# Hybrid decoder step: the mixers' pauses in units 0, 1 and 7, a late copy of scalars, and the order of small column tiles

## The chip, the cores and the metric

The kernel runs on one core of a Trainium2 chip. A core has TensorE (PE, matrix products; its weight loads are listed as PEld), VectorE (DVE), ScalarE (ACT), GpSimd (POOL) and SyncE (SP, which here issues nearly all transfers). Each runs its own list of instructions in order and waits on semaphores for the others. The metric is the device time of one execution in microseconds; of several runs the median counts.

## What is computed

One layer of a decoder, for 16 learned tokens with 256 prompt tokens, and for 8 single sample tokens that go on from given states: T = 280 columns in all, 264 without the learned tokens.

```python
x = LN1(alpha * x + 0.5 * swiglu(x, f1))          # 2048 -> 5504 -> 2048
x = LN2(alpha * x + mixer(x))
x = LN3(alpha * x + 0.5 * swiglu(x, f2))

# mixer: x @ w_in (2048 -> 10 * 2048), split in q_r, k_r, v_r, g_r, q_h, f, i_h, g_h, a_r, a_h
# retention, 8 heads of 256: rotary q, k; decay gamma_h per step
S_new = gamma * S + k^T v ;  o_r = decayed (q k^T) v + q S
# HGRN2 (gated attention), 16 heads of 128: forget gate f per feature, k = 1 - f
S_new = f * S + k^T v ;      o_h = decayed (q k^T) v + q S
y = (sigmoid(a_r) * silu(g_r) * LN(o_r) + sigmoid(a_h) * silu(g_h) * RMS(o_h)) @ w_out
```

Outputs are y for prompt and sample, and the states of both mixers for both.

## The kernel before

**Products.** Features lie on the 128 partitions, tokens are the moving columns. Each number is split in a high and a low part of a reduced float type, and each 128 x 128 weight block takes three matmuls in `dense` (L217): xh·whi, xl·whi, xh·wlo, in this order. Weights are streamed in units of 8 blocks (512 KB): SP loads `raw` (L184), ScalarE rounds it to `whi` (L187), VectorE subtracts to get `wlo` (L188). raw, whi and wlo have three buffers each, so a weight unit is prepared when PE has left the third before it. A unit is 24 matmuls of L217.

**Stages.** FFN 1 (up, dn); the mixer; the output projection (wo); FFN 2. In the mixer the input projection goes in eight units u = 0 to 7, each with two HGRN2 heads and one retention head: the groups f, q_h, i_h, q_r, k_r, v_r of unit u, and then the gates (g_r with a_r, g_h with a_h, for two column blocks) of unit u − 1. After the gates of unit 7 comes wo.

**The two mixers as threads.** What follows a projection is written as two Python generators, `mix_hg(u)` for HGRN2, started after i_h of unit u, and `mix_ret(u)` for retention, started after v_r. `pump` runs once in each k step of a projection (6 matmuls of L217) and advances the threads: `yield n` means that the thread pauses n steps. So a mixer's small matmuls, its pieces, are strewn between projection matmuls, and what other engines do for them hides behind the projections, if the pause is long enough. PE's order is exactly the order in which this program is written. The orders of VectorE, ScalarE, GpSimd and SP are set by the scheduler of the framework: a pause in PE's order moves their instructions too, and they run in that order whatever is ready.

**mix_hg**, in the order of its pieces: transposes of v (pt, L834; `ends`, two copies by GpSimd at L737, L738, is transposed at L837); `blocks` (L808, L810), products of 32 columns of K with Q, the finest levels of the decayed q k^T, on four column tiles of PE (tile positions 0, 32, 64, 96); then for s = 16, 32 (L872) and 64 (L867) the coarser levels (pl). After each level VectorE multiplies K and Q by running products T of f (`mul`, L239), and the next level reads K and Q. Then transposes of K (ptk, L902) with km (L254), and the update of the sample's states smh: ScalarE scales (L908), VectorE adds (L909), 16 of each; the state products (pst), the sample's output (pq), the outputs (po) and their norm (pv).

**mix_ret:** transposes of v and k (pt, L1000, L1009), their split into vs and ks (L1015); scores (psc, L1027; dtab); the state products of both halves c (psr, L1056); then the sample update: the states smr are scaled by ScalarE (L1073) and VectorE adds v·k in 16 instructions (L1078), half e = 0 and half e = 1 with 8 each. Their `vbr` is a row of v in DRAM that SP loads to all partitions (L1044), four loads of two rows, in two buffers. The scalars are columns of the projection k (k_r). A GpSimd memset (L1069) fills the factor for half 1. Then the sample's output (pqr, L1091; osr is centred, L976 to L978), the outputs (por, L1106, and L729) and their norm (pvr, L236).

`calm` adds steps to the pauses: two in units 0 to 6 but not in 1 for mix_hg (which has two in some places by `2 * (u == 1)`), two in units 0 to 6 for mix_ret, none in unit 7.

Of the kernel before, what the change touches and what calls it, by code (L numbers as in the profile page):

```python
# [14 lines left out]
ALU = mybir.AluOpType  # L15
# [3 lines left out]
P = 128  # L19
# [4 lines left out]
NMETA, SEQ, NS = 16, 256, 8  # L24
LP = NMETA + SEQ
# [3 lines left out]
HR, HG = 8, 16  # L29
# [19 lines left out]
W_LEVEL = 6  # L49
# [78 lines left out]
def trunk(ctx: ExitStack, tc: tile.TileContext, A, O):  # L128
    nc = tc.nc
# [416 lines left out]
    with tc.tile_pool(name="yp", bufs=1) as yp:  # L546
# [7 lines left out]
        with tc.tile_pool(name="mp", bufs=1) as mp:  # L554
# [177 lines left out]

            def mix_hg(u, f, k, q, v):

                calm = 2 if u != 1 and u < HR - 1 else 0
                ends = tmp("ends", (P, 2, 2, NMETA))
                nc.gpsimd.tensor_copy(ends[:, :, 0, :], v[:, :, :NMETA])  # L737
                nc.gpsimd.tensor_copy(ends[:, :, 1, :], v[:, :, T - NMETA :])  # L738
# [1 line left out]
                K = tmp("K", (P, 2, LP))  # L740
# [57 lines left out]
                def blocks(x, s, own=None):  # L798

                    x = x.rearrange("p i (x j c) -> p i x j c", x=4, j=4)  # L800
                    for h in range(2):
                        pl = mx_bank("pl")
                        half = pl[:, : 2 * 80].rearrange("p (b c) -> p b c", b=2)
                        for b in range(2):
                            for j in range(0, P, 32):
                                kk = K[:, h, NMETA + b * P + j : NMETA + b * P + j + 32]
                                o = half[j : j + 32, b, :48].rearrange("p (i c) -> p i c", i=3)
                                nc.tensor.matmul(o, kk, x[:, :, 2 * h + b, j // 32, :], start=True, stop=True, tile_position=(0, j))  # L808
                                if own is not None:
                                    nc.tensor.matmul(  # L810
                                        half[j : j + 32, b, 48:], kk, own[:, h, b * P + j : b * P + j + 32],
                                        start=True, stop=True, tile_position=(0, j))
                        a = acc[:, 2 * P * h : 2 * P * (h + 1)]
                        if own is not None:
                            nc.vector.tensor_tensor(
                                out=a.rearrange("p (b j c) -> p b j c", b=2, j=4),
                                in0=half[:, :, 48:].unsqueeze(2).to_broadcast([P, 2, 4, 32]),
                                in1=ident.rearrange("p (j c) -> p j c", j=4).unsqueeze(1).to_broadcast([P, 2, 4, 32]), op=ALU.mult)
                        for i, (sl, mi) in enumerate(((s, MASKS[s][0]), (2 * s, MASKS[2 * s][0]), (2 * s, MASKS[2 * s][1]))):
                            n = 16 // sl  # L820
                            nc.vector.copy_predicated(
                                a.rearrange("p (b j n t s) -> p b j n t s", b=2, j=4, t=2, s=sl)[:, :, :, :, 1, :],
                                msk[:, mi, :P].rearrange("p (b j n s) -> p b j n s", b=2, j=4, s=sl),
                                half[:, :, 16 * i : 16 * i + 16].rearrange("p b (n s) -> p b n s", s=sl).unsqueeze(2).to_broadcast([P, 2, 4, n, sl]))
# [31 lines left out]
                    scale_k(s)  # L856
                scale_q(8)
                join(8)
                yield W_LEVEL + 4 + 2 * (u == 1) + calm
                for s in LEVELS[MASKED:]:  # L860
                    pl = mx_bank("pl")
                    for h in range(2):
                        for b in range(2):
                            k0, q0, o = NMETA + b * P, b * P, (2 * h + b) * s
                            if s == 64:
                                j = 64 * b
                                nc.tensor.matmul(  # L867
                                    pl[j : j + s, h * s : (h + 1) * s], K[:, h, k0 : k0 + s], Q[:, h, q0 + s : q0 + 2 * s],
                                    start=True, stop=True, tile_position=(0, j))
                            else:  # L870
                                for j in range(0, P, 2 * s):
                                    nc.tensor.matmul(  # L872
                                        pl[j : j + s, o : o + s], K[:, h, k0 + j : k0 + j + s],
                                        Q[:, h, q0 + j + s : q0 + j + 2 * s], start=True, stop=True, tile_position=(0, j))
# [13 lines left out]
                    if s in (16, 32):  # L888
                        load(s // 32)
                    yield W_LEVEL + 2 * (u == 1) + calm  # L890
                Tt = Ts[2 * LEVELS[-1]]
                on = tmp("on_h", (P, 2, TL), bufs=2)
                on_h[u] = on
# [86 lines left out]
            def mix_ret(u, q, k, v):  # L980
                vt = tmp("vtr", (P, 2, 2, P))

                ks, vs = (tmp(n, (P, 2, 2, 2 * P), dt=F32R, bufs=4, tag="smr") for n in ("ks", "vs"))
                calm = 2 if u < HR - 1 else 0
                sms = []

                def load(e):
# [62 lines left out]
                for c in range(2):  # L1050
# [6 lines left out]
                    so = tmp("sro", (P, 256))  # L1057
                    nc.scalar.copy(so.rearrange("p (c f) -> p c f", c=2), apart(pst[:, :256]))
                    nc.sync.dma_start(O["srp"][u, c], so)
                    yield 2  # L1060
                load(1)

                centre(vt.rearrange("p b c f -> p b (c f)"))
# [1 line left out]
                centre(vlast.unsqueeze(1))  # L1065
                upper_lower_upper(vs2.rearrange("p c f -> p (c f)"), vlast)

                gams.append(tmp("sro", (P, 1)))
                nc.gpsimd.memset(gams[1], GAMMA[u])  # L1069
                for e in range(2):  # L1070
                    ss = sms[2 * e : 2 * e + 2]
                    for sm in ss:
                        nc.scalar.activation(sm, sm, AF.Copy, scale=gams[e])  # L1073
                    for i in (2 * e, 2 * e + 1):
                        for c in range(2):
                            for b in (2 * i, 2 * i + 1):
                                x, t = ss[c][:, b - 4 * e, :], LP + b
                                nc.vector.scalar_tensor_tensor(  # L1078
                                    out=x, in0=vbs[i][:, b - 2 * i, :], scalar=k[:, c, t : t + 1], in1=x, op0=ALU.mult, op1=ALU.add)
                        spread(i + 2)  # L1080
                    for c in range(2):
                        nc.sync.dma_start(O["srs"][u, c, :, 4 * e : 4 * e + 4, :], ss[c])
                    yield 1 + 5 * (1 - e)
# [173 lines left out]
```

## Time and profile before

| | us |
|---|---|
| median of 3 runs | 2599.12 (2597.02 to 2599.78) |
| profiled execution | 2593.9 |
| its span | 2592.1 |
| PE busy | 2570.6 |
| VectorE busy | 1703.8 |
| ScalarE busy | 1374.9 |
| GpSimd busy | 19.6 |
| granted TensorE clock | 0.999 |

The profiled execution is shorter than the median by 5.2 us. Times of rows count from the start of the span. A matmul's end is modelled, and matmuls overlap, so PE counts as idle only where a row carries a bracket: [time idle <- what ended it]. In the timelines several like instructions in a row are one line with their count. A row of a weight unit names `pj_` and the projection that PE was in.

### The profile page before, as it was taken

The page shows a single profiled execution, that of the slowest core. Times are in us where ns is not written, and L with a number is a line of the kernel's source. Part 1 is how long each engine was busy: PE and PEld are TensorE (multiplying, and loading weights), DVE is VectorE, ACT ScalarE, POOL GpSimd, SP SyncE. Part 2 cuts the span into 40 slices and gives each one's busy share as a digit, 9 for nine tenths or more (in the row PEclk, how much of TensorE's full clock was granted, in tenths as well). Part 3 has the DMA queues.
Part 4 walks back from the last instruction along what each step waited for, and adds up shares of the span by engine and source line. Part 5 has one row for each costly group of instructions (what it writes and reads, how often), then busy time and mean ns, then how long its engine had stood idle before and what let it go on. Part 6 is the DMA issues. An engine that isn't in the chain of part 4 may idle for free.

```text
span 2592.1 us, 56133 instructions
## 1 busy us (share of the span) xinstructions
PE 2570.6 (99%) x23400; PEld 2543.1 (98%) x23400; DVE 1703.8 (66%) x2859; ACT 1374.9 (53%) x2160; POOL 19.6 (1%) x78
## 2 busy tenths in 40 slices
PE   9999999999999999999999999999999999999999
PEld 9999999999999999999999999999999999999998
DVE  6544444565579787777787878786985555556555
ACT  5444444444456665757575757574564444444444
POOL 0000000000000000000000000000000000000000
PEclk9999999999999999999999999999999999999999
DMA  7555555555566786767676767666656666666664
GB/s 242 187 184 184 186 183 184 187 180 186 185 200 208 243 277 208 256 213 253 216 250 219 254 212 253 213 225 195 194 186 199 196 195 196 195 196 194 197 195 148
DMA packets 156895, 536.25 MB, mean 207 GB/s; under 512 B 17952, under 2 KB 25952, under 8 KB 156640
## 3 DMA queue, kind: packets, MB, share of 16 engines
q1 hardware_dynamic: 156352, 532.37, 63.2%
q8 instruction: 183, 3.00, 0.5%
q14 instruction: 72, 0.59, 0.1%
q10 hardware_dynamic: 288, 0.29, 0.0%
HBM read 501.99 MB, written 30.61 MB: 205 GB/s over the span
## 4 chain that ended last, share of the span: by engine, by line
PE 59%; DVE 1%; ACT 1%; issue 0%; POOL 0%; DVEq 0%; ACTq 0%; POOLq 0%
PE up L217 17%; PE dn L217 9%; PE wo L217 3%; PE pj_g_r L217 3%; PE pj_g_h L217 3%; PE pj_a_h L217 3%; PE pj_k_r L217 3%; PE pj_a_r L217 3%; PE pj_v_r L217 3%; PE pj_q_r L217 2%; PE pj_i_h L217 2%; PE pj_f L217 2%; PE pj_q_h L217 2%; DVE wlo L188 0%; PE pqr L1091 0%; PE por L1106 0%
## 5 line engine op out<-in xcount | busy, mean ns | idle before, releaser
L188 DVE TENSOR_TENSOR wlo<-raw,whi 128x1024 fp32r<-128x1024 f32 (+1 forms) x869 | 1062.8, 1223 | 762.1 <-ACT whi L187 760.5
L187 ACT CAST whi<-raw 128x1024 fp32r<-128x1024 f32 (+1 forms) x870 | 905.6, 1042 | 938.1 <-PE up L217 419.2
L217 PE MATMUL up<-xh,whi 128*128 128x280 f32 (+1 forms) x2624 | 725.6, 280 | 0.8 <-ACT whi L187 0.8
L217 PE MATMUL up<-xh,wlo 128*128 128x280 f32 (+1 forms) x2624 | 725.8, 280 | 0.4 <-DVE wlo L188 0.4
L217 PE MATMUL up<-xl,whi 128*128 128x280 f32 (+1 forms) x2624 | 725.4, 279 | 0.0
L217 PEld LDWEIGHTS up<-xh,whi 128*128 128x128 f32 x2624 | 492.6, 189 | 1.0 <-ACT whi L187 1.0
L217 PEld LDWEIGHTS up<-xh,wlo 128*128 128x128 f32 x2624 | 492.6, 189 | 1.0 <-DVE wlo L188 1.0
L217 PEld LDWEIGHTS up<-xl,whi 128*128 128x128 f32 x2624 | 492.6, 189 | 0.0
L217 PE MATMUL dn<-hh,whi 128*128 128x280 f32 (+1 forms) x1376 | 384.7, 280 | 0.0
L217 PE MATMUL dn<-hl,whi 128*128 128x280 f32 (+1 forms) x1376 | 384.3, 279 | 0.0
L217 PE MATMUL dn<-hh,wlo 128*128 128x280 f32 (+1 forms) x1376 | 384.3, 279 | 0.0
L217 PEld LDWEIGHTS dn<-hh,whi 128*128 128x128 f32 x1376 | 260.1, 189 | 0.1
L217 PEld LDWEIGHTS dn<-hl,whi 128*128 128x128 f32 x1376 | 260.1, 189 | 0.1
L217 PEld LDWEIGHTS dn<-hh,wlo 128*128 128x128 f32 x1376 | 260.1, 189 | 0.0
L217 PE MATMUL pj_g_r<-xh,whi 128*128 128x264 f32 x256 | 76.8, 300 | 0.0
L217 PE MATMUL pj_k_r<-xh,whi 128*128 128x280 f32 x256 | 73.7, 288 | 0.0
L217 PE MATMUL pj_g_h<-xh,whi 128*128 128x264 f32 x256 | 73.6, 288 | 0.0
L217 PE MATMUL pj_v_r<-xh,whi 128*128 128x280 f32 x256 | 73.5, 287 | 0.0
L217 PE MATMUL pj_v_r<-xh,wlo 128*128 128x280 f32 x256 | 72.4, 283 | 0.3 <-DVE wlo L188 0.3
L217 PE MATMUL pj_k_r<-xh,wlo 128*128 128x280 f32 x256 | 72.4, 283 | 0.0
L217 PE MATMUL pj_v_r<-xl,whi 128*128 128x280 f32 x256 | 72.3, 283 | 0.0
L217 PE MATMUL pj_k_r<-xl,whi 128*128 128x280 f32 x256 | 72.3, 283 | 0.0
(396 smaller groups left out, 5230.3 us busy)
## 6 DMA issues: line engine op xcount, KB each, us to landing
raw<-in_w_up SPq DMA_DIRECT2D x343, 512.0 KB
raw<-in_w_in SPq DMA_DIRECT2D x320, 512.0 KB
raw<-in_w_dn SPq DMA_DIRECT2D x172, 512.0 KB
smr<-in_sr SPq DMA_DIRECT2D x32, 512.0 KB
out_srs<-smr SPq DMA_DIRECT2D x32, 512.0 KB
raw<-in_w_out SPq DMA_DIRECT2D x32, 512.0 KB
smh<-in_sg SPq DMA_DIRECT2D x16, 512.0 KB
vbr<-vrd SPq DMA_DIRECT2D x32, 256.0 KB
```

The costliest lines, as they stand in the source:

```text
L187: nc.scalar.copy(hi[:, j:jn, :], raw[:, j:jn, :])
L188: nc.vector.tensor_tensor(out=lo[:, j0:j1, :], in0=raw[:, j0:j1, :], in1=hi[:, j0:j1, :].bitcast(F32), op=ALU.subtract)
L217: nc.tensor.matmul(o, w, t, start=start, stop=stop)
```

## The change

Five things change. In `mix_hg` calm is 2 in all units: unit 1, which had two more steps only at the coarser levels, has them at every pause, and so has unit 7 (unit 0 goes without at its last pauses, as before). In `mix_ret` calm is 2 in all units. In unit 0 mix_ret waits ten steps instead of two after the second state product. The eight scalars of the sample update's second half are copied by GpSimd into a small tile behind the memset, and half 1 reads the copy. And `blocks` issues for each b the four products of 48 columns first and then the four of 32 columns.

```diff
-                calm = 2 if u != 1 and u < HR - 1 else 0
+                calm = 2
...
-                            for j in range(0, P, 32):
-                                kk = K[:, h, NMETA + b * P + j : NMETA + b * P + j + 32]
-                                o = half[j : j + 32, b, :48].rearrange("p (i c) -> p i c", i=3)
-                                nc.tensor.matmul(o, kk, x[:, :, 2 * h + b, j // 32, :], start=True, stop=True, tile_position=(0, j))
-                                if own is not None:
+                            for mine in range(1 if own is None else 2):
+                                for j in range(0, P, 32):
+                                    at = b * P + j
+                                    o, y = half[j : j + 32, b, :48].rearrange("p (i c) -> p i c", i=3), x[:, :, 2 * h + b, j // 32, :]
+                                    if mine:
+                                        o, y = half[j : j + 32, b, 48:], own[:, h, at : at + 32]
                                     nc.tensor.matmul(
...
-                yield W_LEVEL + 4 + 2 * (u == 1) + calm
+                yield W_LEVEL + 4 + calm
...
-                    yield W_LEVEL + 2 * (u == 1) + calm
+                    yield W_LEVEL + calm
...
-                calm = 2 if u < HR - 1 else 0
+                calm = 2
...
-                    yield 2
+                    yield 2 if u or c == 0 else 10
...
-                gams.append(tmp("sro", (P, 1)))
+                late = tmp("sro", (P, 1 + NS))
+                gams.append(late[:, :1])
                 nc.gpsimd.memset(gams[1], GAMMA[u])
+                late_k = late[:, 1:].rearrange("p (c b) -> p c b", c=2)
+                nc.gpsimd.tensor_copy(late_k, k[:, :, LP + 4 :])
...
+                                kk = late_k[:, c, b - 4 : b - 3] if e else k[:, c, t : t + 1]
                                 nc.vector.scalar_tensor_tensor(
-                                    out=x, in0=vbs[i][:, b - 2 * i, :], scalar=k[:, c, t : t + 1], in1=x, op0=ALU.mult, op1=ALU.add)
+                                    out=x, in0=vbs[i][:, b - 2 * i, :], scalar=kk, in1=x, op0=ALU.mult, op1=ALU.add)
```

VectorE in unit 0, from the weight subtract at 841.62 us on. wlo is a weight subtract; L1078 (L1082 in the changed kernel) adds a term to the sample's retention states; K and Q are scaled by T of level 16 for PE's products of level 32. Before:

```order
L188 TENSOR_TENSOR wlo_10091<-raw_10089,whi_10090 128x8x128
L1078 SCALAR_TENSOR_TENSOR smr<-vbr,k_r,smr 128x256
L188 TENSOR_TENSOR wlo_10128<-raw_10126,whi_10127 128x8x128
L1078 SCALAR_TENSOR_TENSOR smr<-vbr,k_r,smr 128x256 x4
L188 TENSOR_TENSOR wlo_10177<-raw_10175,whi_10176 128x8x128
L1078 SCALAR_TENSOR_TENSOR smr<-vbr,k_r,smr 128x256 x3
L239 TENSOR_TENSOR K<-K,T_9897 128x2x8x16
L239 TENSOR_TENSOR Q<-Q,T_9897 128x16x16
L188 TENSOR_TENSOR wlo_10207<-raw_10205,whi_10206 128x8x128
```

After:

```order
L188 TENSOR_TENSOR wlo_10080<-raw_10078,whi_10079 128x8x128
L1082 SCALAR_TENSOR_TENSOR smr<-vbr,sro,smr 128x256
L188 TENSOR_TENSOR wlo_10129<-raw_10127,whi_10128 128x8x128
L239 TENSOR_TENSOR K<-K,T_9897 128x2x8x16
L239 TENSOR_TENSOR Q<-Q,T_9897 128x16x16
L1082 SCALAR_TENSOR_TENSOR smr<-vbr,sro,smr 128x256 x2
L188 TENSOR_TENSOR wlo_10178<-raw_10176,whi_10177 128x8x128
L1082 SCALAR_TENSOR_TENSOR smr<-vbr,sro,smr 128x256 x5
L188 TENSOR_TENSOR wlo_10208<-raw_10206,whi_10207 128x8x128
```

K and Q have moved ahead of seven instructions of the sample update and of a weight subtract. The first of the second half's instructions (now with its scalar in sro) stands between the same two subtracts as before.

VectorE in unit 1, from 942.16 us on; K and Q are scaled for the levels 16 (after only; before, this pair stands further up) and 32. Before:

```order
L1078 SCALAR_TENSOR_TENSOR smr<-vbr,k_r,smr 128x256 x4
L188 TENSOR_TENSOR wlo_11585<-raw_11583,whi_11584 128x8x128
L1078 SCALAR_TENSOR_TENSOR smr<-vbr,k_r,smr 128x256
L239 TENSOR_TENSOR K<-K,T_11368 128x2x4x32
L239 TENSOR_TENSOR Q<-Q,T_11368 128x8x32
L188 TENSOR_TENSOR wlo_11626<-raw_11624,whi_11625 128x8x128
L1078 SCALAR_TENSOR_TENSOR smr<-vbr,k_r,smr 128x256 x4
```

After:

```order
L239 TENSOR_TENSOR K<-K,T_11226 128x2x8x16
L239 TENSOR_TENSOR Q<-Q,T_11226 128x16x16
L225 TENSOR_TENSOR yl_8612<-y,yh_8609 128x264
L254 TENSOR_TENSOR vs_8641<-vt_8636,vs_8641 24x256
L1082 SCALAR_TENSOR_TENSOR smr<-vbr,k_r,smr 128x256 x3
L188 TENSOR_TENSOR wlo_11587<-raw_11585,whi_11586 128x8x128
L1082 SCALAR_TENSOR_TENSOR smr<-vbr,k_r,smr 128x256 x2
L188 TENSOR_TENSOR wlo_11617<-raw_11615,whi_11616 128x8x128
L1082 SCALAR_TENSOR_TENSOR smr<-vbr,sro,smr 128x256 x4
L239 TENSOR_TENSOR K<-K,T_11421 128x2x4x32
L239 TENSOR_TENSOR Q<-Q,T_11421 128x8x32
L188 TENSOR_TENSOR wlo_11658<-raw_11656,whi_11657 128x8x128
```

The sample update has moved back against the weight subtracts and against K and Q: the pair of level 32 (with 2x4x32 and 8x32 elements) stood behind five instructions of the first half and now stands behind the first four of the second. The pair of level 16 has come down behind the subtract that ran at 939.39 us.

VectorE in unit 7, in retention's split of k (ks) with the scores (dtab). km and smh belong to HGRN2. Before:

```order
L1015 SCALAR_TENSOR_TENSOR ks_8640<-pt,dec,ks_8640 24x128
L254 TENSOR_TENSOR vs_8641<-vt_8636,vs_8641 24x128
L1015 SCALAR_TENSOR_TENSOR ks<-pt,dec,ks 128x128
L254 TENSOR_TENSOR km<-ptk,km 16x128
L909 SCALAR_TENSOR_TENSOR smh<-vbh,fk,smh 128x128 x2
L1015 SCALAR_TENSOR_TENSOR ks<-pt,dec,ks 128x128
L909 SCALAR_TENSOR_TENSOR smh<-vbh,fk,smh 128x128 x5
L239 TENSOR_TENSOR dtab<-psc,dtab 128x400
L188 TENSOR_TENSOR wlo_22358<-raw_22356,whi_22357 128x8x128
L1015 SCALAR_TENSOR_TENSOR ks_8640<-pt,dec,ks_8640 24x128
```

After:

```order
L188 TENSOR_TENSOR wlo_22247<-raw_22245,whi_22246 128x8x128
L1015 SCALAR_TENSOR_TENSOR ks_8640<-pt,dec,ks_8640 24x128
L1015 SCALAR_TENSOR_TENSOR ks<-pt,dec,ks 128x128
L239 TENSOR_TENSOR dtab<-psc,dtab 128x400
L239 TENSOR_TENSOR K<-K,T_22022 128x2x2x64
L1015 SCALAR_TENSOR_TENSOR ks_8640<-pt,dec,ks_8640 24x128
```

HGRN2's instructions have left this stretch; the pair of level 64 has come into it. The rows after are those of units 2 to 6.

PE's own list changes in `blocks` as the diff says, and in where the pieces stand among the projection matmuls: in unit 0 pqr and the por pieces stand 48 matmuls of L217 later than before; in unit 1 L872 and L867 and the ptk pieces 24 later, pst 36 later, por and pqr at the same place; in unit 7 all pieces stand where they stand in unit 6.

More of the change, by code (lines that the diff above doesn't have):

```diff
@@ L804, in blocks @@
                         for b in range(2):
-                            for j in range(0, P, 32):
-                                kk = K[:, h, NMETA + b * P + j : NMETA + b * P + j + 32]
-                                o = half[j : j + 32, b, :48].rearrange("p (i c) -> p i c", i=3)
-                                nc.tensor.matmul(o, kk, x[:, :, 2 * h + b, j // 32, :], start=True, stop=True, tile_position=(0, j))
-                                if own is not None:
+                            for mine in range(1 if own is None else 2):
[4 more added lines that the diff above has]
+                                        o, y = half[j : j + 32, b, 48:], own[:, h, at : at + 32]
                                     nc.tensor.matmul(
-                                        half[j : j + 32, b, 48:], kk, own[:, h, b * P + j : b * P + j + 32],
-                                        start=True, stop=True, tile_position=(0, j))
+                                        o, K[:, h, NMETA + at : NMETA + at + 32], y, start=True, stop=True, tile_position=(0, j))
                         a = acc[:, 2 * P * h : 2 * P * (h + 1)]
```

## The prediction

> **What bounds the kernel now.** I read the page's first part, then the table of waits for TensorE, then the windows of single units, and last the timelines of VectorE and TensorE around the places found.
>
> ```profile
> span 2592.1 us, 56133 instructions
> PE 2570.6 (99%) x23400; PEld 2543.1 (98%) x23400; DVE 1703.8 (66%) x2859; ACT 1374.9 (53%) x2160; POOL 19.6 (1%) x78
> ```
>
> TensorE (PE) is busy 99% of the span. The change neither removes nor adds a matmul, so only the idle rest can be won: 2592.1 − 2570.6 = 21.5 us, less what lies at the two ends. The table of waits says who holds PE (total, times, longest):
>
> ```profile
> PE pl L872 <- DVE Q L239: 2.4, 1, 2.4
> PE por L729 <- ACT yh L224: 1.8, 1, 1.8
> PE psr L1056 <- DVE ks L1015: 1.5, 1, 1.5
> PE ptk L902 <- DVE K L239: 1.4, 1, 1.4
> PE pj_i_h L217 <- DVE wlo L188: 1.3, 1, 1.3
> PE pj_q_h L217 <- DVE wlo L188: 1.1, 1, 1.1
> PE pvr L236 <- DVE rlo L225: 0.8, 1, 0.8
> PE ptk L902 <- DVE km L254: 0.6, 1, 0.6
> PE pvr L236 <- ACT rhi L224: 0.4, 1, 0.4
> ```
>
> Each occurs once. No wait repeats eight times, so the kernel doesn't wait in every unit but in a few. The windows tell which: a steady unit (number 5 of 0 to 7), then the same stretch of the projections, from the start of i_h on, in units 6 and 7.
>
> ```profile
> core 0: us, PE busy (x) PEld busy (x) DVE busy (x) ACT busy (x) POOL busy (x), PEclk, DMA share, GB/s
> 1407.00:1535.50 128.50, 128.50 (x1274) 125.83 (x1273) 98.42 (x199) 82.33 (x154) 1.64 (x5) 1.00 0.70 234
> 1507.00:1613.00 106.00, 106.00 (x1078) 103.25 (x1077) 80.15 (x164) 64.24 (x129) 1.64 (x5) 1.00 0.73 245
> 1635.50:1745.50 110.00, 106.74 (x1079) 103.37 (x1078) 84.51 (x175) 69.55 (x138) 4.46 (x16) 1.00 0.70 227
> ```
>
> In units with the long pauses PE never stops. Unit 7, without them, loses 110.00 − 106.74 = 3.26 us, at the granted clock 1.00 in both.
>
> **Unit 7: long pauses.** The psr, ptk<-km and both pvr waits (1.5 + 0.6 + 0.8 + 0.4) are this 3.3. The largest, on both engines:
>
> ```profile
> 1698.02 0.35 DVE L1015 SCALAR_TENSOR_TENSOR ks<-pt,dec,ks 128x128 fp32r<-128x128 f32 x1
> 1698.28 1.39 DVE L909 SCALAR_TENSOR_TENSOR smh<-vbh,fk,smh 128x128 f32<-128x128 f32 x5
> 1701.33 0.34 DVE L1015 SCALAR_TENSOR_TENSOR ks<-pt,dec,ks 24x128 fp32r<-24x128 f32 x1
> 1701.72 0.38 PE L1056 MATMUL psr<-vs,ks 128*128 128x256 f32 x1 [1.48 <-DVE ks L1015]
> ```
>
> Between two of retention's ks instructions stand five of gated attention's sample update: short pauses let both mixers run into one another. The order of the changed kernel has none between them, and its VectorE rows of unit 7 are those of unit 6, whose window shows no idle PE. VectorE, ScalarE and the weights do the same work in both. So I take −3.3. The ends: −3.3 is all that is idle there, 0 if the waits only move. The matmuls themselves move among the projections and cost what they cost.
>
> **Unit 0: the sample update eight steps on.**
>
> ```profile
> 845.84 0.48 DVE L1078 SCALAR_TENSOR_TENSOR smr<-vbr,k_r,smr 128x256 f32<-128x256 f32 x1 [3.00 <-DMA vbr<-vrd]
> 846.24 1.22 DVE L188 TENSOR_TENSOR wlo<-raw,whi 128x1024 fp32r<-128x1024 f32 x1
> 847.37 1.67 DVE L1078 SCALAR_TENSOR_TENSOR smr<-vbr,k_r,smr 128x256 f32<-128x256 f32 x4
> 848.96 1.22 DVE L188 TENSOR_TENSOR wlo<-raw,whi 128x1024 fp32r<-128x1024 f32 x1
> 850.09 1.27 DVE L1078 SCALAR_TENSOR_TENSOR smr<-vbr,k_r,smr 128x256 f32<-128x256 f32 x3
> 851.28 0.42 DVE L239 TENSOR_TENSOR K<-K,T 128x256 f32<-128x256 f32 x1
> 851.62 0.42 DVE L239 TENSOR_TENSOR Q<-Q,T 128x256 f32<-128x256 f32 x1
> 852.09 0.45 PE L872 MATMUL pl<-Q,K 128*32 128x32 f32 x16 [2.40 <-DVE Q L239]
> 853.52 0.28 PE L217 MATMUL pj_i_h<-xh,wlo 128*128 128x280 f32 x1
> ```
>
> PE wants Q at 852.09 − 2.40 = 849.69, but seven updates and a weight subtract stand ahead of K and Q. In the changed order K and Q come right behind the subtract of 846.24, so Q ends near 847.37 + 0.34 + 0.42 = 848.1, before 849.69: −2.4. What is late next: the subtract of 848.96, which ended at 850.18, has K, Q and two updates ahead instead of four updates and ends no later; PE reaches its product at 853.52 − 2.40 = 851.1, so 0.9 us are left, and the subtracts behind it do the same work in the same time. The first update, which waits 3.00 for its load, stands where it stood, ahead of the subtract; so the waits of 1.1 and 1.3 on wlo (pj_q_h, pj_i_h) stay. Between −2.4 and −1.4 (−4.8 if they went too), I take −2.4, the row's own wait.
>
> **Unit 1: longer pauses.** Its own price is in no row, so I place the new order on the old times.
>
> ```profile
> 942.68 0.33 SPq L1044 DMA_DIRECT2D vbr<-vrd  x1
> 945.28 0.43 DVE L239 TENSOR_TENSOR K<-K,T 128x256 f32<-128x256 f32 x1
> 945.61 0.43 DVE L239 TENSOR_TENSOR Q<-Q,T 128x256 f32<-128x256 f32 x1
> 948.14 1.67 DVE L1078 SCALAR_TENSOR_TENSOR smr<-vbr,k_r,smr 128x256 f32<-128x256 f32 x4 [0.97 <-DMA vbr<-vrd]
> 946.27 0.45 PE L867 MATMUL pl<-Q,K 128*64 128x64 f32 x8
> 945.17 0.28 PE L217 MATMUL pj_a_r<-xh,whi 128*128 128x264 f32 x1
> 945.28 0.28 PE L217 MATMUL pj_a_r<-xl,whi 128*128 128x264 f32 x1
> 953.77 0.55 PE L902 MATMUL ptk<-ident,K 128*128 128x128 f32 x3 [1.45 <-DVE K L239]
> ```
>
> L867 and ptk move 24 projection matmuls on; at 0.11 us from one to the next (945.17 to 945.28) that is 2.7 us. That covers ptk's wait of 1.45 for K: gone. But K and Q for L867 now stand behind four updates of the sample's second half, which wait for a load. It was issued at 942.68 and in by 948.14, 5.46 us later, and the queue ahead of its issue is as full as before. So Q ends at 949.73 (948.14 and the four updates' 1.67, overlapping) + 0.34 + 0.42 = 950.5; PE wants it at 946.27 + 2.7 = 949.0: a new wait of 1.5, or 2.7 if the load is issued a subtract's 1.22 later, since updates and subtracts have changed places ahead of it. An earlier K and Q pair, moved between two subtracts (0.34 each), may make a subtract up to 0.7 late. −1.45 + 1.5 to 2.7 + 0 to 0.7: 0 to +1.9, of which I take +0.5, nearer the end that the rows give. The por wait of 1.8 stays: its place among the projections is the same. Bounds: −3.2 (it goes with ptk's, none new) and +5 (the load in full, 5.46, instead of ptk's wait, and the subtract).
>
> [...]
>
> **Column tiles in turn.** The block with both widths, and one of the 48 alone:
>
> ```profile
> 1016.59:1017.43 0.84, 0.84 (x32) 0.72 (x32) 1.00 1.03 376
> 1026.93:1027.40 0.47, 0.47 (x32) 0.41 (x32) 1.00 1.05 410
> ```
>
> The windows count L808 alone (32 matmuls of 48 columns); the first holds as many of 32 columns beside. At the cost per column of the plain block both would take 0.47 × 80/48 = 0.78; at its cost per matmul 0.94. At 0.84 the alternating order already runs within these ends, so there are −0.06 to +0.10 in each of eight blocks: −0.5 to +0.8. I take 0, what the row shows.
>
> **The late copy.** GpSimd gets eight copies of 128 x 8:
>
> ```profile
> 867.26 0.98 POOL L737 COPY ends<-v 128x32 f32<-128x32 f32 x1 [7.36 <-ACT v L658]
> 940.39 0.10 POOL L1069 MEMSET sro<- 128x1 f32 x1 [7.58 <-ACT vs L708]
> ```
>
> At up to 1.0 us each, right behind the memset of 940.39, they end by 941.6, when the updates that read them start at 948.14: 0. That cover is 6 us; only if the memset came so much later would VectorE, and the subtracts behind it, wait.
>
> **Sum.** −3.3 − 2.4 + 0.5 + 0 + 0 = −5.2 against the profiled execution, 2593.9 us, that is 2588.7. It ran 5.2 us under the median of the three runs shown (2599.1); against the median I forecast 2593.9.
>
> **Rivals.**
> 1. No new wait in unit 1: the load is in when K and Q are due. For it: unit 6 has the same loads, and PE waits for nothing in its window. Against: the 5.46 of the row. Then ptk's 1.45 is won (−3.3 − 2.4 − 1.45 = −7.2), at best por's 1.8 too (−8.9): 2590 to 2592. [...]
> 2. The gains are partly given back, by L867's 2.7 and the late subtract in unit 1, or by a subtract in unit 0 that PE, 2.4 us sooner, finds unfinished. −3.3 − 1.4 + 1.9 = −2.8 down to nothing: 2596 to 2599.
> 3. Slower: the loads of unit 1's sample update. In the new order a subtract stands behind the first use of each of the four, and VectorE's queue runs in order, so a late load holds up what PE needs next. Each can hold it 5.46 at most, its full time from issue to landing; three of four in full: −5.7 − 1.45 + 16.4 = +9.2, 2608. It decides from 7.2 us of new waits on, and beyond 12.4 it is slower by over 0.2%. Against it: the longest hold of a load in the old order, with the same loads, was 3.00.
> 4. Unit 7's pauses do nothing for psr: −1.9 or less; unlikely, with the order equal to unit 6's. It counts with the second.
>
> **How the numbers follow.** A measurement of this kernel tells about 0.2%, 5.2 us, from no change, so the forecast lies on the border. The forecast's own case (2592 to 2596) 0.50, of which 0.30 beyond the border; rival 1, 0.20, faster; rival 2 with 4, 0.20, the same; rival 3, 0.10, slower. So 0.50, 0.40, 0.10. The range goes from rival 1, with 0.5 from the column tiles and 1.5 more for unit 0's wlo waits (2588), to rival 2's end and a microsecond (2600).
>
> **What would show it.** Right: no psr, pvr or ptk wait in unit 7, and its window from i_h on as long as PE's busy time; no L872 wait in unit 0, the two wlo waits of 1.1 and 1.3 still there; an L867 wait for Q of 1.5 to 2.7 in unit 1, none of ptk; own blocks of 0.8 us. Wrong: waits of unit 7 that turn up elsewhere in it, a wlo wait in unit 0 behind the removed one, or over 3 us new in unit 1.

## The result, and the profile after

The changed kernel takes 2590.47 us (median of 7 runs, 2588.51 to 2591.58) against 2597.69 us for the kernel before on the same chip (7 runs, 2596.27 to 2599.78). The ratio is 0.9971 with the interval [0.9959, 0.9982]: 7.2 us less, 4.7 to 10.7 by the interval. That is faster, by a little more than such a measurement can tell from no change.

The profiled execution of the changed kernel took 2591.02 us, 0.6 above its median; that of the kernel before, 2593.9 us, lay 3.8 below its median of 7. So the two spans differ by only 3.0 us, and the traces are compared wait by wait, not by their ends.

The page's first part, and the table of PE's waits (total, times, longest), of the changed kernel:

```profile
span 2589.1 us, 56134 instructions
PE 2572.7 (99%) x23400; PEld 2545.6 (98%) x23400; DVE 1703.4 (66%) x2859; ACT 1375.6 (53%) x2160; POOL 22.9 (1%) x86
```

```profile
PE pj_i_h L217 <- DVE wlo L188: 2.7, 1, 2.7
PE psr L1056 <- DVE ks L1015: 1.8, 1, 1.8
PE por L729 <- ACT yh L224: 1.8, 1, 1.8
...
PE por L1110 <- DVE sc L254: 0.3, 1, 0.3
```

Of the nine waits quoted from before, pl<-Q, both ptk, both pvr, q_h and unit 7's psr are gone. One of them is back elsewhere: this psr wait is in unit 1. The rows left out (none above 1.0) are outside the units of the change and were there before too. Adding the brackets of the timelines by unit:

| PE waits, us | before | after | difference |
|---|---|---|---|
| unit 0 | 4.77 (q_h 1.06, i_h 1.31, L872 2.40) | 2.67 (i_h) | −2.1 |
| unit 1 | 3.67 (ptk 1.45, por 1.75, one of 0.47) | 3.83 (psr 1.82, por 0.26 and 1.75) | +0.2 |
| unit 7 | 3.27 | 0 | −3.3 |
| all of PE | 15.29 | 10.04 | −5.25 |

**Unit 7** in the changed kernel, from the start of i_h (1636.45) to g_r's first product (1742.31), by windows:

```profile
core 0: us, PE busy (x) PEld busy (x) DVE busy (x) ACT busy (x) POOL busy (x), PEclk, DMA share, GB/s
1636.40:1742.40 106.00, 106.00 (x1080) 103.31 (x1080) 81.02 (x166) 65.15 (x131) 3.10 (x15) 1.00 0.70 235
```

PE no longer stops: 106.00 of 106.00.

**Unit 0.** PE, then VectorE. L1082 is the sample update, the former L1078:

```profile
848.10 0.51 PE L217 MATMUL pj_i_h<-xh,wlo 128*128 128x280 f32 x1 [2.67 <-DVE wlo L188]
848.40 0.44 PE L217 MATMUL pj_i_h<-xh,whi 128*128 128x280 f32 x1
848.63 0.44 PE L217 MATMUL pj_i_h<-xl,whi 128*128 128x280 f32 x1
```

```profile
846.42 0.48 DVE L1082 SCALAR_TENSOR_TENSOR smr<-vbr,sro,smr 128x256 f32<-128x256 f32 x1 [4.36 <-ACT whi L187]
846.82 1.22 DVE L188 TENSOR_TENSOR wlo<-raw,whi 128x1024 fp32r<-128x1024 f32 x1
847.96 0.42 DVE L239 TENSOR_TENSOR K<-K,T 128x256 f32<-128x256 f32 x1
848.29 0.42 DVE L239 TENSOR_TENSOR Q<-Q,T 128x256 f32<-128x256 f32 x1
```

K and Q stand right behind the subtract, as the order said, and PE doesn't wait for them. The first update of the second half holds VectorE's queue 4.36 us here (3.00 in the trace of before). The row names whi, which an update doesn't read; in a repeat of this kernel (below) the same row names the load of `vbr`. The weight subtract behind it is what i_h waits for.

The second thing in this view is the pitch of the matmuls: from 848.40 to 848.63 are 0.23 us instead of the 0.11 to 0.12 of the rest of the stream. The granted clock says why (windows, same columns as above):

```profile
847.22:848.22 1.00, 0.12 (x1) 0.13 (x2) 1.00 (x2) 0.00 (x0) 0.00 (x0) 1.00 0.76 303
848.22:851.63 3.41, 3.41 (x15) 3.41 (x16) 3.41 (x8) 1.34 (x2) 0.00 (x0) 0.50 0.80 209
...
971.10:974.51 3.41, 3.41 (x17) 3.40 (x16) 1.75 (x5) 2.42 (x5) 0.00 (x0) 0.50 0.96 354
```

PE counts as busy in these stretches and does half the work (15 matmuls in the first, where 0.12 us from one to the next would give 28). There are two, of 3.41 us each, one behind the i_h wait and one behind a wait of unit 1, so together they cost up to 2 × 1.7 = 3.4 us in this execution, an estimate from half of each. The profiled execution of before had none.

The weight matmuls come in the same order in both traces, so the same one can be looked up in both:

| first product of | before, us | after, us | difference |
|---|---|---|---|
| the mixer's f | 745.13 | 745.59 | +0.46 |
| unit 3's f, behind the pieces of units 0 and 1 | 1098.78 | 1100.45 | +1.67 |
| unit 7's f | 1612.79 | 1613.98 | +1.19 |
| wo | 1788.78 | 1785.73 | −3.05 |

The stretch with the pieces of units 0 and 1 became 1.2 us longer: −1.9 of waits, −0.3 of three blocks with the new column order (below), and +3.4, which is what the two stretches at half clock cost. From unit 7's f to wo it became 4.2 us shorter, of which the brackets explain 3.3 and one block 0.1; the other 0.9 carries no bracket, and its place wasn't found.

**Unit 1.** PE, VectorE, and the load's issue on SP's queue:

```profile
938.14 0.38 PE L1056 MATMUL psr<-vs,ks 128*128 128x256 f32 x1 [1.82 <-DVE ks L1015]
951.01 0.45 PE L867 MATMUL pl<-Q,K 128*64 128x64 f32 x8
969.83 0.30 PE L729 MATMUL por<-ident,osr 128*128 128x128 f32 x1 [1.75 <-ACT yh L224]
```

```profile
935.39 0.48 DVE L1082 SCALAR_TENSOR_TENSOR smr<-vbr,k_r,smr 128x256 f32<-128x256 f32 x1 [1.73 <-DMA vbr<-vrd]
...
936.51 1.20 DVE L188 TENSOR_TENSOR wlo<-raw,whi 128x1024 fp32r<-128x1024 f32 x1
937.75 0.34 DVE L1015 SCALAR_TENSOR_TENSOR ks<-pt,dec,ks 24x128 fp32r<-24x128 f32 x1
...
947.60 1.67 DVE L1082 SCALAR_TENSOR_TENSOR smr<-vbr,sro,smr 128x256 f32<-128x256 f32 x4 [0.21 <-DMA vbr<-vrd]
949.53 0.42 DVE L239 TENSOR_TENSOR Q<-Q,T 128x256 f32<-128x256 f32 x1
```

```profile
943.96 0.33 SPq L1044 DMA_DIRECT2D vbr<-vrd  x1
```

The new wait that I forecast, L867 for Q, isn't there: the load was in 3.6 us after its issue (943.96 to 947.60), Q was ready at 949.95, and PE came to L867 only at 951.01. Another new wait is: an update of the sample's first half waits 1.73 us for its load ahead of retention's last `ks`, and psr waits 1.82 us for that ks.

**Column tiles.** L811 alone now stands for all 64 matmuls of a unit's own block:

```profile
1018.36:1019.11 0.75, 0.75 (x64) 0.71 (x64) 1.00 1.03 382
```

From the first start to the start of the matmul behind the block it takes 0.750 us, against 0.844 to 0.845 before, in each of the eight: −0.76 us. The scalars' copy by GpSimd in unit 0 ran at 838.49 us, 8 us ahead of the first update that reads it (846.42).

### The profile page after: what moved, and what is told of

Read it like the earlier page. It is cut to its first block, busy times and chain, and to the rows that moved or that the text cites. A ratio compares the mean times of both kernels' runs of the same rounds, so it can differ in the third digit from the quotient of the medians.

```text
span 2589.1 us, 56134 instructions
## 1 busy us (share of the span) xinstructions
PE 2572.7 (99%) x23400; PEld 2545.6 (98%) x23400; DVE 1703.4 (66%) x2859; ACT 1375.6 (53%) x2160; POOL 22.9 (1%) x86
## 4 chain that ended last, share of the span: by engine, by line
PE 93%; DVE 4%; DMA 1%; ACT 1%; issue 1%; SPq 0%; ACTq 0%; DVEq 0%
PE up L217 34%; PE dn L217 18%; PE pj_g_r L217 4%; PE pj_i_h L217 3%; PE pj_a_r L217 3%; PE pj_g_h L217 3%; PE pj_a_h L217 3%; PE pj_k_r L217 3%; PE wo L217 3%; PE pj_v_r L217 3%; PE pj_q_r L217 3%; PE pj_f L217 3%; PE pj_q_h L217 3%; DVE wlo L188 2%; DMA raw<-in_w_up 1%
## 5 line engine op out<-in xcount | busy, mean ns | idle before, releaser
L217 PE MATMUL up<-xh,whi 128*128 128x280 f32 (+1 forms) x2624 | 725.6, 280 | 0.8 <-ACT whi L187 0.8
L217 PE MATMUL up<-xh,wlo 128*128 128x280 f32 (+1 forms) x2624 | 725.9, 280 | 0.4 <-DVE wlo L188 0.3
L217 PE MATMUL up<-xl,whi 128*128 128x280 f32 (+1 forms) x2624 | 725.4, 279 | 0.0
L217 PEld LDWEIGHTS up<-xh,wlo 128*128 128x128 f32 x2624 | 492.6, 189 | 1.3 <-DVE wlo L188 1.3
L217 PEld LDWEIGHTS up<-xh,whi 128*128 128x128 f32 x2624 | 492.6, 189 | 1.0 <-ACT whi L187 1.0
L217 PEld LDWEIGHTS up<-xl,whi 128*128 128x128 f32 x2624 | 492.6, 189 | 0.0
L217 PE MATMUL dn<-hh,whi 128*128 128x280 f32 (+1 forms) x1376 | 384.7, 280 | 0.0
L217 PE MATMUL dn<-hh,wlo 128*128 128x280 f32 (+1 forms) x1376 | 384.3, 279 | 0.0
L217 PE MATMUL dn<-hl,whi 128*128 128x280 f32 (+1 forms) x1376 | 384.3, 279 | 0.0
L217 PEld LDWEIGHTS dn<-hl,whi 128*128 128x128 f32 x1376 | 260.1, 189 | 0.1
L217 PEld LDWEIGHTS dn<-hh,whi 128*128 128x128 f32 x1376 | 260.1, 189 | 0.1
L217 PEld LDWEIGHTS dn<-hh,wlo 128*128 128x128 f32 x1376 | 260.1, 189 | 0.0
L217 PE MATMUL pj_g_r<-xh,whi 128*128 128x264 f32 x256 | 76.5, 299 | 0.0
L217 PE MATMUL pj_g_h<-xh,whi 128*128 128x264 f32 x256 | 73.8, 288 | 0.0
L217 PE MATMUL pj_k_r<-xh,whi 128*128 128x280 f32 x256 | 73.8, 288 | 0.0
L217 PE MATMUL pj_v_r<-xh,whi 128*128 128x280 f32 x256 | 73.4, 287 | 0.0
L217 PE MATMUL pj_v_r<-xh,wlo 128*128 128x280 f32 x256 | 72.4, 283 | 0.3 <-DVE wlo L188 0.3
L217 PE MATMUL pj_k_r<-xh,wlo 128*128 128x280 f32 x256 | 72.4, 283 | 0.0
L217 PE MATMUL pj_v_r<-xl,whi 128*128 128x280 f32 x256 | 72.3, 283 | 0.0
L217 PE MATMUL pj_k_r<-xl,whi 128*128 128x280 f32 x256 | 72.3, 283 | 0.0
```

The lines of the kernel that those rows point to most:

```text
L217: nc.tensor.matmul(o, w, t, start=start, stop=stop)
```

## Experiments

The first four make one part of the change alone, beside 33 runs of the kernel before (median 2595.83 us).

**Unit 7 alone.**

```diff
-                calm = 2 if u != 1 and u < HR - 1 else 0
+                calm = 2 if u != 1 else 0
...
-                calm = 2 if u < HR - 1 else 0
+                calm = 2
```

> The kernel before with the long pauses in unit 7 alone. Theory of waits: unit 7 loses its waits psr, ptk and pvr, and nothing else changes: -3.3 us, with the unit's window from i_h on about 106.7 us instead of 110.0. Rival, the waits only move within unit 7: 0, other waits there of 3 us in sum. Rival, the unit's waits also cost a slower TensorE clock behind them in most executions: -4 to -6 in the median, with the same -3.3 in the table of waits.

Measured: 2592.63 us, ratio 0.9986 [0.9978, 0.9995], 3.2 us less. Unit 7 by windows, and the one wait of PE in 1600 to 1780:

```profile
1639.40:1745.40 106.00, 105.36 (x1072) 102.49 (x1071) 80.19 (x163) 64.45 (x129) 2.56 (x14) 1.00 0.69 234
```

```profile
PE pj_g_r L217 <- DVE wlo L188: 0.6, 1, 0.6
```

The psr, ptk and pvr waits are gone. The 0.6 left is one late weight subtract, which the profile of the whole change doesn't have. Unit 7 is the only part whose gain is seen by itself in the time.

**Unit 0 alone.**

```diff
-                    yield 2
+                    yield 2 if u or c == 0 else 10
```

> The kernel before with unit 0's sample update eight steps on alone. Theory of waits: L872's wait of 2.4 for Q goes, the two wlo waits in q_h and i_h together stay at 2.4 to 2.7: -2.1 to -2.4 us. Rival, the clock: the one longer wlo wait of 2.7 in place of two short ones halves the granted clock for about 3.5 us behind it, which costs 1.7, so -0.7 us, with PE pitches of 234 ns instead of 117 behind 848 us.

Measured: 2594.67 us, 0.9994 [0.9985, 1.0003]: 1.2 us less, not told from none. The first of PE's waits from 820 to 880, and the second one's rows on PE and VectorE:

```profile
PE pj_i_h L217 <- DVE wlo L188: 1.4, 1, 1.4
```

```profile
870.68 0.30 PE L729 MATMUL por<-ident,osr 128*128 128x128 f32 x1 [1.34 <-ACT whi L187]
```

```profile
868.02 1.22 DVE L188 TENSOR_TENSOR wlo<-raw,whi 128x1024 fp32r<-128x1024 f32 x1 [1.02 <-ACT whi L187]
...
870.11 0.42 DVE L978 TENSOR_TENSOR osr<-osr,cen 128x256 f32<-128x256 f32 x1
```

L872's 2.40 is gone and a por wait is new: PE, sooner by it, finds osr not yet centred. In the whole change VectorE has the same order there, and the same row has no wait, since PE comes to it 2.67 us and thirteen slow matmuls late:

```profile
872.66 0.30 PE L729 MATMUL por<-ident,osr 128*128 128x128 f32 x1
```

So what is left in unit 0 is one debt that falls due at i_h or at por: 1.41 + 1.34 = 2.75 us here, 2.67 in the whole change, against 4.77 before, which is −2.0. One pair of traces says too much, though: with unit 0's order of before, these waits come to 3.3 to 4.9 us in five traces (before, and the runs with unit 7, unit 1, the column order and the crossed tiles; 4.2 on average), and with the new order to 2.5 to 2.8 in four (2.6). So the part is worth about −1.6, and L872's own wait, which the prediction priced at 2.40, was 1.0 to 2.4.

**Unit 1 alone.**

```diff
-                calm = 2 if u != 1 and u < HR - 1 else 0
+                calm = 2 if u < HR - 1 else 0
...
-                yield W_LEVEL + 4 + 2 * (u == 1) + calm
+                yield W_LEVEL + 4 + calm
...
-                    yield W_LEVEL + 2 * (u == 1) + calm
+                    yield W_LEVEL + calm
```

> The kernel before with the long pauses in unit 1 alone. Prediction's step: ptk's 1.45 goes, L867 waits 1.5 to 2.7 for Q: +0.5 (0 to +1.9). As the profile after shows it: no L867 wait, but psr waits 1.8 for ks, ptk and the wait for ends (0.5) go, por stays: 0 to +0.3.

Measured: 2595.82 us, 0.9998 [0.9989, 1.0007]. PE's waits from 905 to 1012:

```profile
PE por L729 <- ACT yh L224: 1.7, 1, 1.7
PE por L1106 <- DVE sc L254: 1.1, 1, 1.1
PE psr L1056 <- DVE ks L1015: 1.1, 1, 1.1
```

3.9 us instead of 3.67: ptk's wait goes, psr's comes, none at L867. Unit 1's part gives nothing, in the time and in the trace.

**Column order alone**, the diff of `blocks` as in the change.

> The kernel before with the order of the column tiles alone. Prediction's step: 0, within -0.5 to +0.8. From the profile after: each of eight blocks takes 0.75 us instead of 0.845: -0.8 us, too little for the median to show; the rows show it. No wait changes.

Measured: 2595.72 us, 0.9996 [0.9987, 1.0004]. The block takes what it takes in the whole change:

```profile
1016.62:1017.37 0.75, 0.75 (x64) 0.71 (x64) 1.00 1.07 415
```

A gain of 0.75 us is seen in the trace and is too small to be told in the time. The four parts add to −0.14 − 0.06 − 0.02 − 0.04 = −0.26%, the whole gave −0.29%: they act side by side, as far as these intervals can tell.

The next four start from the changed kernel, beside 15 runs of the kernel before (2596.9 us).

**The changed kernel again**, with no edit.

> The changed kernel once more. Its profile showed PE at half pitch (234 ns from matmul to matmul) behind two of its waits, which the profile of the kernel before did not. If that hangs on the waits alone, the same two places show it again (unit 0 in i_h behind a wait of 2.7, unit 1 behind por's 1.8), if it hangs also on where the wait falls in the clock's own rhythm, it comes and goes between executions with waits of like length. Sum of the single parts by medians: 0.9974 of the kernel before, so 0.997 here.

Measured: 2590.53 us, 0.9977 [0.9967, 0.9986]. PE's waits from 820 to 980, and unit 0 on VectorE:

```profile
PE pj_i_h L217 <- DVE wlo L188: 2.5, 1, 2.5
PE por L729 <- ACT yh L224: 1.8, 1, 1.8
PE psr L1056 <- DVE ks L1015: 0.9, 1, 0.9
```

```profile
845.52 0.48 DVE L1082 SCALAR_TENSOR_TENSOR smr<-vbr,sro,smr 128x256 f32<-128x256 f32 x1 [4.17 <-DMA vbr<-vrd]
```

The same waits, and here the row names the load as what unit 0's update waits for. The half clock came back behind the same two waits, i_h and por, again for 3.41 us each.

**Without the late copy.**

```diff
-                late = tmp("sro", (P, 1 + NS))
-                gams.append(late[:, :1])
+                gams.append(tmp("sro", (P, 1)))
...
-                late_k = late[:, 1:].rearrange("p (c b) -> p c b", c=2)
-                nc.gpsimd.tensor_copy(late_k, k[:, :, LP + 4 :])
...
-                                kk = late_k[:, c, b - 4 : b - 3] if e else k[:, c, t : t + 1]
+                                kk = k[:, c, t : t + 1]
```

> The changed kernel without the late copy (the second half reads k again). Prediction's step: the copy costs nothing and hides, so 0 against the changed kernel, and VectorE's order is the same but for that operand. Rival: the copy frees k of the unit early, and without it the next unit's k waits: +1 or more, as waits of VectorE's rot or k_r behind the sample update.

Measured: 2589.75 us, 0.9973 [0.9962, 0.9984], within the interval of the one before it; PE's waits from 820 to 980 are those of the changed kernel (i_h 2.7, por 1.8, psr 0.9). The copy neither wins nor costs anything that can be measured.

**Unit 0's pause longer still.** The update that waits for the load goes twelve steps further back, and so does the load's own issue (838.88 us in the repeat, 842.34 here):

```diff
-                    yield 2 if u or c == 0 else 10
+                    yield 2 if u or c == 0 else 22
```

> The changed kernel with 22 steps instead of 10 in unit 0. In VectorE's order the second half's first update now stands behind the next weight subtract and behind K and Q. Theory (the load's landing holds up the subtract): the i_h wait of 2.7 goes, and with it the half pitch behind it: -2.5 to -4 us against the changed kernel. Rival: the wait only moves to por or to a later subtract of unit 0: 0.

Measured: 2587.22 us, 0.9962 [0.9950, 0.9975], 3.3 us below the repeat of the changed kernel, though the two intervals overlap. PE's waits from 820 to 980:

```profile
PE por L729 <- ACT yh L224: 1.8, 1, 1.8
PE pj_q_h L217 <- DVE wlo L188: 0.7, 1, 0.7
PE psr L1056 <- DVE ks L1015: 0.6, 1, 0.6
```

The i_h wait is gone, and with it the half clock at 848 us: 2.5 − 0.7 = 1.8 of waits and up to 1.7 of half clock, 3.5 together. The one behind por is still there. No update stands between the subtracts of 841 and 843 us any more, and the first of the second half, at 847.48, waits for nothing: that an update waiting for its load ahead of the subtract made i_h wait is shown by moving it away.

**And longer pauses in unit 1**, ahead of psr and ahead of por, on top of the last:

```diff
-                yield 4
+                yield 8 if u == 1 else 4
...
-                yield 7
+                yield 11 if u == 1 else 7
```

> As e7, and in unit 1 four steps more ahead of retention's state products and of its outputs. Theory: psr finds its ks (1.8 saved) and por its centred osr (1.8 saved), with the half pitch behind it: -3 to -5 us against e7, -6 to -9 against the changed kernel, 0.994 of the kernel before. Rival: unit 1's update of the sample moves along and its loads hold up a subtract instead: -1 or less against e7.

Measured: 2588.59 us, 0.9966 [0.9954, 0.9979]. PE's only larger wait from 820 to 980:

```profile
PE ptk L902 <- DVE K L239: 2.4, 1, 2.4
```

psr and por don't wait any more, but nothing is won by it (the intervals of this run and the last overlap): K of level 64 now stands behind eight sample updates, and ptk waits for it. That is the wait that unit 1 had before the change, longer.

The last two stand beside 9 runs of the kernel before (2597.03 us).

**Only the second of those two pauses**, again on unit 0's 22 steps:

```diff
-                    yield 2 if u or c == 0 else 10
+                    yield 2 if u or c == 0 else 22
...
-                yield 7
+                yield 11 if u == 1 else 7
```

> As e7, and in unit 1 four steps more ahead of retention's outputs only. Theory: por's wait of 1.75 for the centred osr goes and ptk keeps its K, since the sample update hasn't moved: -1.8 us against e7, or -2.5 with the half pitch behind it. Rival: the outputs' norm behind por is now late for pvr or for the gates of unit 1: 0 or more.

Measured: 2583.90 us (2583.53 to 2585.96), 0.9951 [0.9938, 0.9965]. Its span, and PE's waits from 820 to 980:

```profile
span 2581.8 us, 56126 instructions
```

```profile
PE psr L1056 <- DVE ks L1015: 1.2, 1, 1.2
PE pj_i_h L217 <- DVE wlo L188: 0.8, 2, 0.4
```

por's wait is gone and ptk's stays away. Over the whole span PE's brackets come to 6.0 us (15.3 before, 10.0 in the changed kernel), and no stretch at half clock is left. Its span is 7.3 us shorter than that of the changed kernel's profile: 4.0 of brackets and 3.4 of half clock. By the medians this version is faster than the kernel before by 13 us, and than the changed kernel by 6.6 (2590.5 in both of its measurements, at 0.9971 and 0.9977 of the kernel before).

**Column tiles crossed.** The order of before, in which a product of 48 columns and one of 32 alternate, but with the second on another of the four column tiles, so that no two neighbours share one:

```diff
+                                    i = (j + 64) % P
...
-                                        half[j : j + 32, b, 48:], kk, own[:, h, b * P + j : b * P + j + 32],
-                                        start=True, stop=True, tile_position=(0, j))
+                                        half[i : i + 32, b, 48:], K[:, h, NMETA + b * P + i : NMETA + b * P + i + 32],
+                                        own[:, h, b * P + i : b * P + i + 32], start=True, stop=True, tile_position=(0, i))
```

> The kernel before, with 48 and 32 columns still in alternation, but each product of 32 columns on the column tile two further on, so that no two matmuls in a row stand on the same tile. If the alternating block lost its time because two matmuls in a row had the same tile, it takes 0.75 us like the changed one; if it lost it by changing between the widths, 0.845 like the one before. In both cases 0 to -0.8 us, which one look can't tell from no change.

Measured in one execution: 2596.97 us. The window counts L808 alone, as the prediction's row of 0.84 did:

```profile
1019.95:1020.71 0.76, 0.76 (x32) 0.69 (x32) 1.00 1.04 307
```

The widths still alternate, and the block takes 0.76 all the same (0.753 to 0.754 in all eight, from the first start to the start of the matmul behind). So it isn't the mixing of widths that cost 0.09 us, but two matmuls in a row on the same column tile, or that such a pair reads the same block of K, which the crossed order ends too.

## Why the prediction was right, and where it wasn't

The forecast of −5.2 us against the profiled execution lies in the measured interval (−4.7 to −10.7), and 2590.5 lies in the range; the case "faster by over 0.2%" came true by 0.09%. But it isn't the forecast's own case (2592 to 2596) that the time fell into, and the sum held partly by luck: several of its terms were off, on both sides, and the profile after holds 3.4 us of half clock that it didn't have. Against the median of 7 runs shown since (2597.69) the same −5.2 would have been 2592.5: of the 3.4 us by which 2593.9 missed, 1.4 are the median of three runs that I set out from, and 2.0 are the change itself. Of these the column tiles explain 0.8. The waits and the blocks together come to −6.0 (−3.3 − 2.1 + 0.2 − 0.8), with unit 7's 0.9 that carries no bracket to −6.9. The half clock isn't in this sum: it comes and goes between executions, with unit 0's order of before too, and how often it was in the runs behind the medians isn't known. What is left lies within the interval.

- **Unit 7, −3.3.** Right in its cause, and somewhat small. The window shows PE busy throughout, the part alone measured −3.2. By the same weight matmuls in both traces the unit became 4.2 us shorter: "cost what they cost" put the matmuls' new places at nothing, and 0.9 lies there or in waits without a bracket. That the rows of VectorE were those of unit 6 carried it.
- **Unit 0, −2.4.** Right in mechanism, and a little too large: L872's wait went, and 2.5 to 2.8 us stay instead of the 2.4 of "the two waits on wlo". I took both to stay as they were. In fact q_h's went and i_h's grew, because one load decides it: its hold of VectorE was 3.00 in the trace that I read and 4.36 in the profile after, on instructions at the same place. That isn't the change's doing: the hold is 2.8 to 4.6 in five traces with the old order and 3.1 to 4.4 in four with the new, and where it is long, i_h waits longer in both. The step that failed is that durations which a transfer sets, and L872's 2.40 that hangs on them, were taken as fixed from one execution.
- **Unit 1, +0.5.** The number is near (+0.2), the step behind it wrong. I forecast "a new wait of 1.5, or 2.7" at L867, from the load's 5.46 us; that load took 3.6, and PE came late enough by psr's own wait. It wasn't the one execution: in five traces with unit 1's old order this load takes 5.2 to 6.9 us, in six with the new order 3.6 to 4.7. So a duration read from the old order doesn't hold for the new one. The new wait is psr's, 0.6 to 1.8 us long in six executions (the profile after, its repeat, and the runs with unit 1 alone, without the copy, with unit 0's longer pause, and with por's), and it comes from the place I had named only in the third rival, an update of the first half with its load ahead of what PE needs. Unit 1's rows as I quoted them start behind that place, and I did not look further up. That por's 1.8 stays and ptk's 1.45 goes was right.
- **Rival 1**, no new wait in unit 1, gave 2590 to 2592, and the time fell there, but its reason did not hold: L867's wait stayed away, and psr's took its place. The rows show its load in after 3.6 us here and 5.46 before.
- **Column tiles, 0, bounds −0.5 to +0.8.** −0.76: outside the bounds. The lower bound let the whole 0.47 us of the plain block grow with its columns, but part of a block is fixed. With 0.478 = a + 32 × 48 × c and 0.750 = a + 32 × 80 × c, a is 0.07 us and c 0.27 ns a column, an estimate from these two, so the block could come down to 0.75, not 0.78. And the row of 0.84 I read as the price of mixed widths, where it held a price of the order (the crossed tiles show that it isn't the widths).
- **The late copy, 0.** Right.
- **Rival 2** (given back) happened in unit 0 alone, where 1.34 of por's wait came behind the one removed, and with the longer pauses ahead of both psr and por, where ptk's came back; in the whole change it is hidden behind the i_h wait. **Rival 3** named the right kind of place in both units, and a size that wasn't reached: the holds were 1.73 and 4.36, not 5.46 on three of four.
- **Not in the prediction at all:** the half clock. It cost up to 3.4 us in the profile after, and as much in its repeat.

What stays open: why one load of the second half holds VectorE between 2.8 and 4.6 us in nine traces with the same or nearly the same order was not followed to the queue; the runs show only that with load and update twelve steps later the update finds its rows there. Why unit 1's load is faster in the new order, and where unit 7's 0.9 us lie, stay open too.

## What to carry to other kernels

VectorE runs its list in order here: an instruction that waits for a load held all that stands behind it, 4.36 us in unit 0, and PE paid at the next thing it needed from that list (2.67 at i_h), whatever that is called in the table of waits; so when pauses are moved, read the list above and below the place, and find each instruction that waits for a transfer. A duration that a transfer sets wants several executions and a range, not one row (unit 0's hold was 2.8 to 4.6 us in nine traces), and a row of the old order may not hold for the new one at all (5.46 before, 3.6 after). And a removed wait is worth its row only up to the next thing that is late: in unit 0 one of 2.4 us was worth about 1.6, in unit 1 one of 1.45 was worth nothing, until the pause was put ahead of the right piece.

## What the runs showed of the hardware

**A half clock behind short waits.** After some waits PE's matmuls of 280 columns start 0.233 us apart instead of 0.119 (848.40 to 851.43 and 99.83 to 102.93 in the profile after), and the granted clock is 0.50. Each such stretch lasts 3.41 us (in the run with crossed tiles 6.83, twice that). Small matmuls slow down with the rest: from the first of por's four products (L1110) to the matmul behind them it is 1.17 us in such a stretch (969.54 to 970.71 in the repeat) and 0.59 without (967.38 to 967.97 in the fastest version).

Like waits differ. The wait of 2.40 us ahead of L872 is followed by such a stretch in the run with unit 1 alone, and by none in the trace of before. First the run with unit 1 alone, then before:

```profile
848.41:851.82 3.41, 1.01 (x22) 0.76 (x21) 3.41 (x7) 1.07 (x3) 0.00 (x0) 1.00 0.92 341
851.82:855.23 3.41, 3.41 (x15) 3.41 (x16) 3.20 (x8) 1.54 (x3) 0.00 (x0) 0.50 1.00 318
```

```profile
847.86:851.27 3.41, 1.83 (x16) 1.62 (x14) 3.41 (x7) 1.34 (x2) 0.00 (x0) 1.00 0.86 281
851.27:854.68 3.41, 2.59 (x34) 2.55 (x35) 3.38 (x10) 1.56 (x3) 0.00 (x0) 1.00 0.99 362
```

Where a trace has two stretches, their starts lie a whole number of steps of 3.413 us apart (122.88 us, 36 steps, in the profile after; 119.47, 35 steps, in its repeat; 119.46, 35 steps, with unit 1 alone). In the profile after, the first starts a whole number of such steps (247, 843.09 us) behind the point where the trace's record of the clock begins, 5.13 us into the span. The windows above are such steps, for before counted from that point (4.77 us). With unit 1 alone the whole 2.40 lies in one step, and the next runs at half clock; in before it lies across a border, 1.58 and 0.82.

Counted so, by the brackets of PE, the profile after has two steps that are followed by a half clock, with 2.67 and 1.89 us of waits (por's 1.75 and 0.14 of the 0.26 ahead of it); the fullest of its others holds 1.17. In before the fullest step holds 1.75, and none is followed by a half clock. These are counts in single executions; what sets the clock isn't shown by them, and no run was made to find out.

Each stretch costs up to 1.7 us, an estimate from half of its 3.41, so the wait of 2.40 us was followed by nearly as much again in one trace and by nothing in the other.

**The order of small matmuls on column tiles.** 64 matmuls of 32 and 48 columns took 0.845 us when each pair ran on one column tile, and 0.750 to 0.754 when neighbours ran on different ones, in either order of widths.

**A load's time under a stream of weights.** The same 256 KB load of unit 1 took 5.2 to 6.9 us from issue to landing in five traces with the old order and 3.6 to 4.7 in six with the new. The loads ahead of it in SP's queue are the same; in the old order it is issued 1.2 us behind a 512 KB load of states, in the new order 1.8 us (942.13 to 943.96 in the profile after). Whether that makes the difference isn't shown.
